# A fused decoder layer on one core: a pause of the gathers at the gates, residual rows fetched eight chunks earlier, first turns of u ahead of the last scores

## The chip, the cores and the metric

The kernel runs on one core of a Trainium2 chip, as one program. The metric is the time of one execution on the device in microseconds (us), the median of three runs. The core has five engines that the text names: TensorE (PE, matrix products), VectorE (DVE), ScalarE (ACT), GpSimd (POOL) and SyncE (SP, which here only starts transfers). Each of them issues its instructions in the order of the program; a transfer is issued on the queue of one of them and waits there, with all that stands behind it, until what it needs is ready.

## The reference, cut to what matters

One decoder layer over 256 tokens of width 1024, all in float32: a mixer (chunkwise retention and block attention, merged by gates, with an output projection and a residual add), then a retrieval of experts by product keys.

```python
def peer(h, w_q, sub_keys, u_tab, v_tab):
    q = (ht @ w_q).reshape(T, PEER_HEADS, 2, half)
    s = jnp.einsum('thcd,hcnd->thcn', q, sub_keys).astype(jnp.float32)
    s1, i1 = lax.top_k(s[:, :, 0], PEER_TOPK)
    s2, i2 = lax.top_k(s[:, :, 1], PEER_TOPK)
    ...
    top_s, pos = lax.top_k(cand_s, PEER_TOPK)
    experts = jnp.take_along_axis(cand_i, pos, axis=-1)
    gates = jax.nn.softmax(top_s, axis=-1).astype(h.dtype)
    ...
        u = u_tab[ec]
        a = jax.nn.gelu(jnp.einsum('td,thkd->thk', hc, u), approximate=False)
        return jnp.einsum('thk,thkd->td', gc * a, v_tab[ec])
...
def reference(x, ...):
        ...
        x = x + merged @ w_out[l]
        h2 = rmsnorm(x, ffn_norm_g[l])
        x = x + peer(h2, peer_w_q[l], peer_sub_keys[l], peer_u[l], peer_v[l])
```

There are 8 heads, 128 x 128 = 16384 experts with a row of `peer_u` and a row of `peer_v` each (1024 wide, 64 MB per table), and every token takes 16 experts per head.

## The kernel before, in words

The order of the work is written by hand: the program's order is each engine's order. Generators (`tasks`, `chain`) are advanced by fixed budgets between the products of PE, so that side work falls between them.

**Stages.** To about 275 us the mixer runs. Then four units of the query projection follow, each of them with an epilogue (`queries`, L567) that copies the queries to SBUF on ScalarE (L571), multiplies them by the sub-keys on PE (L580, a `side` tile of PSUM for each half of the tokens) and copies the scores out on ScalarE (L584). From there VectorE works through the choice of the best experts (`topk`).

**The tables in chunks.** Both tables are streamed whole through SBUF in 128 chunks of 128 experts (512 KB each), since 192 of the tokens are treated densely. A chunk of u is turned by 8 transposes on PE (L675, `transpose_u`; ScalarE evacuates, L676), two chunks ahead of its use (`TAHEAD`), and then multiplied with the tokens (L1178). This runs from 315 to about 695 us. The chunks of v are cut in two parts of the product's format (L141 on ScalarE gives the high part `rhi`, L142 on VectorE the remainder `rlo`) two chunks ahead, the weights likewise (`cut_w`, L1149 on ScalarE, L1150 on VectorE, every second chunk), and `block` (L1211, L1212) multiplies and sums into eight PSUM banks, one for each 128 of the output's columns, until about 985 us.

**Dense gates** (`dense_gates`, L1075). For the dense product each token needs a weight for each expert: for the 16 x 8 chosen ones the gate, else zero. The columns of chosen indices and gates are turned on PE (`columns`, L1084; ScalarE copies, L1085 and L1086); for four tokens at a time VectorE builds two sets of one-hots (L1063, `oh_buf`; L1065, `oh_more`), ScalarE scales one of them by the gates in four `factors` (L1069), and PE multiplies them (L1105, `gp`). VectorE and ScalarE evacuate the result into `W` (L1118, L1120). The generator says by `yield` how much of a budget each step costs; the main loop gives `BUDGET` 1.5 per chunk. The first group's products come two groups behind its one-hots (`LAG_G`).

**Gathers** (`gather_step`, L994). The experts' rows of 64 tokens, and the u rows of 64 more ("extra" tokens), are gathered by indirect transfers on POOL's queue (`fetch`, L942), one row per partition, into five buffers. VectorE takes the dot product of a u row (L953) one step after it is taken from the ring. For v it adds the weighted row to `vacc` (L1023). The main loop calls for 1.08 steps per chunk of u and 0.54 per chunk of v. The extra tokens' weights then go out and back through memory by POOL's queue (L964 `gx`, L969 `gates`), since the second `columns` call needs them in another layout.

**The end.** At chunk 120 (`NK - 8`) the remaining sums of gathered rows are done, and the residual rows of the first 64 tokens are loaded by ScalarE's queue (L1231) and added (L1235, L1237). At chunk 125 SP's queue stores these (L1238) and loads the other residual rows (L1241) into two buffers of the ring that otherwise holds the streamed chunks. Then, for each of the eight banks, ScalarE and VectorE add the two halves (L1248, L1249), PE turns the result back (L1254, L1255), VectorE adds the residual rows (L1256, L1257), and the result is stored (L1260, L1261).

Of the kernel before, what the change touches and what calls it, by code (L numbers as in the profile page):

```python
# [22 lines left out]
P = 128  # L23
# [20 lines left out]
BUDGET = 1.5  # L44
GSTEP = 1.6
LAG_G = 2
SCRATCH = 88
TOPK = 16
HELD = [0, 1, 2] + list(range(8, 62, 6))
# [19 lines left out]
def layer_kernel(ctx, tc, x, mix_norm_g, w_in, ret_w_branch, moba_q_gain, moba_k_gain, moba_w_branch,  # L69
# [21 lines left out]
    def side():  # L91
        return psum["side"].tile([P, 512], F32, name="side")
# [474 lines left out]
    def queries(q):  # L567
        def epi(o):
            qT = scratch[:, 4096:5120].rearrange("p (j t) -> p j t", j=4)
            for b in range(2):  # L570
                A.activation(qT[:, 2 * b:2 * b + 2, :], o[b].rearrange("p (a t) -> p a t", a=2), AF.Copy)  # L571
            yield
            if q == 0:
                yield
                yield
                assert sk_task not in tasks
            for t in range(NT):
                p = side()
                for j in range(4):
                    T.matmul(p[:, j * P:(j + 1) * P], qT[:, j, t * P:(t + 1) * P], skT[:, 4 * q + j, :],  # L580
                             start=True, stop=True)
                n0 = 512 * (2 * q + t)
                s_sb = scratch[:, n0:n0 + 512].rearrange("p (j i) -> p j i", j=4)
                A.activation(s_sb, p.rearrange("p (j i) -> p j i", j=4), AF.Copy, scale=r2[:, t:t + 1])  # L584
                (chain if t == 0 else topk_rest).append(topk(t, q, s_sb))
            yield
        return epi
# [77 lines left out]
    def transpose_u(c):  # L665

        if c < NK and c % STEP == STEP - 1 and c // STEP < NPRE:
            u_T[c] = u_raw.pop(c)
        elif c < NK:
            r = u_raw.pop(c)  # L670
            u_T[c] = hi_tile(F32)
            for q in range(2):
                p = psum["turn"].tile([P, 512], F32, name="turn")
                for k in range(4):
                    T.transpose(p[:, k * P:(k + 1) * P], r.rearrange("p (i k) -> p k i", k=KC)[:, 4 * q + k], ident)  # L675
                A.activation(u_T[c][:, 512 * q:512 * (q + 1)], p, AF.Copy)  # L676
# [145 lines left out]
            V.max_index(idx[:, 8:16], vals[:, 8:16], tmp)  # L822


    gs = {"n": 0, "u": 0, "dot": 0, "v": 0, "sum": 0, "rows": {}, "x": 0, "soft": False, "xdone": False, "later": []}

    topk_rest = []
    ready = []
# [164 lines left out]

    def gather_step():  # L994
        later()
        if gs["x"] == NX and gs["soft"]:
            weights_x()
        if gs["dot"] < NU:
            if gs["u"] < len(ready):
                fetch(peer_u[0], ready[gs["u"]])  # L1000
                gs["u"] += 1
            if gs["dot"] < gs["u"] and (gs["u"] - gs["dot"] == RING - 1 or gs["u"] == NU):
                j = ready[gs["dot"]]
                r = gs["rows"].pop(j)
                h = h2 if j < NJ else h2r[(j - NJ) // TOPK]
                after(1, partial(dot_v, j, r, h))
                gs["dot"] += 1
                if gs["dot"] == NU:
                    later()
                    A.activation(av[:, :NJ], av[:, :NJ], AF.Gelu)  # L1010
                    V.tensor_tensor(av[:, :NJ], av[:, :NJ], gg[:, :NJ], op=OP.mult)
            return
        if gs["v"] < NJ:
            fetch(peer_v[0], gs["v"])
            gs["v"] += 1
        if gs["sum"] < gs["v"] and (gs["v"] - gs["sum"] == RING or gs["v"] == NJ):
            j = gs["sum"]
            r = gs["rows"].pop(j)
            if j == 0:
                gs["acc"] = cp.tile([P, D], F32, name="vacc", tag="h2")  # L1020
                A.activation(gs["acc"], r, AF.Copy, scale=av[:, 0:1])
            else:
                V.scalar_tensor_tensor(gs["acc"], r, av[:, j:j + 1], gs["acc"], op0=OP.mult, op1=OP.add)  # L1023
            gs["sum"] += 1

    held = list(HELD)

    def hold():
# [50 lines left out]
    def dense_gates():  # L1079
# [5 lines left out]
            A.activation(tT[:, t], p[:, P:3 * P].rearrange("p (j i) -> p j i", j=2), AF.Copy)  # L1085
            A.activation(tT1[:, t], p[:, :P], AF.Copy)  # L1086

        yield 5.0
        columns(1)
        yield 0.1  # L1090
        V.tensor_scalar(niota, iota, -1.0, None, op0=OP.mult)
        oh_buf = cp.tile([P, 4, 4, NK], F32, name="oh_buf", tag="b8")
        V.tensor_copy(iota4, iota[:, :, None].to_broadcast([P, NK, 4]))
        built = []
        for n0 in range(0, ND + 4 * LAG_G, 4):
            gates_finish()
# [61 lines left out]
            h2r.append(lo_tile(F32))  # L1158
            nc.scalar.dma_start(h2r[n], h2y[n].rearrange("h i d -> (h i) d"))

    for c in range(TAHEAD):
        transpose_u(c)
    for c in range(NK):
        load_to(len(pieces) + c + TAHEAD)
        rows_x(c)
# [37 lines left out]

    o = [acc() for _ in range(KC)]
    half = P - NG
    res, late = {}, []

    def block(b, c):
        vh, vl, w = cuts[c]
# [5 lines left out]
    for c in range(NK):  # L1215
# [10 lines left out]
        if c == NK - 8:  # L1226
# [4 lines left out]
            nc.scalar.dma_start(r0[:NG], x1d[:NG, 0, :])  # L1231
            upper = hp_.tile([P, D], F32, name="rows", tag="hh", bufs=2)
            nc.gpsimd.dma_start(upper[:NG], gs["acc"][NG:])
        if c == NK - 4:
            V.tensor_tensor(r0[:NG], r0[:NG], gs["acc"][:NG], op=OP.add)  # L1235
        if c == NK - 3:
            V.tensor_tensor(r0[:NG], r0[:NG], upper[:NG], op=OP.add)  # L1237
            nc.sync.dma_start(out_flat[:NG, :], r0[:NG])  # L1238
            for i, src in enumerate((x1d[NG:, 0, :], x1d[:, 1, :])):
                res[i] = raw_tile()  # L1240
                nc.sync.dma_start(res[i][:src.shape[0]], src)  # L1241

    r0b, r1 = res[0], res[1]
    back = {}

    def add_up(b):
# [77 lines left out]
```

## Time and profile before

| what | value |
|---|---|
| three runs | 999.03, 1001.88, 1005.34 us; median 1001.88 |
| the profiled execution | 1003.14 us, span 1001.4 us (1.74 around it), mean granted clock of PE 0.992 |
| busy in the span | PE 984.5 (98%), VectorE 803.6 (80%), ScalarE 551.4 (55%), POOL 331.8 (33%) |
| moved | 309.94 MB, mean 310 GB/s |

The span is cut into the stretch before the u phase and so on by the table of windows; these are its rows, with the busy time of PE, its weight loads, VectorE, ScalarE and POOL (in brackets the count of instructions), then the granted clock, the share of the transfer engines and GB/s:

```
0.00:275.00 275.00, 272.64 (x1676) 239.43 (x1677) 190.02 (x247) 137.47 (x209) 35.13 (x41) 1.00 0.80 240
275.00:309.00 34.00, 33.93 (x280) 33.14 (x279) 29.17 (x137) 13.82 (x18) 1.77 (x3) 1.00 0.99 381
309.00:502.00 193.00, 187.07 (x1672) 186.29 (x1670) 174.08 (x603) 87.89 (x175) 96.77 (x89) 1.00 0.98 371
502.00:575.00 73.00, 73.00 (x630) 73.00 (x631) 62.17 (x108) 54.35 (x159) 36.93 (x35) 0.96 0.88 320
575.00:695.00 120.00, 119.47 (x1072) 119.28 (x1071) 83.89 (x140) 94.81 (x238) 56.46 (x58) 1.00 0.86 318
695.00:984.00 289.00, 289.00 (x2017) 289.00 (x2018) 258.11 (x254) 160.43 (x190) 104.73 (x62) 1.00 0.91 333
984.00:1001.40 17.40, 9.41 (x50) 8.27 (x48) 6.14 (x25) 2.65 (x8) 0.00 (x0) 0.75 0.36 105
```

In the rows of the time line that follow below, the first two numbers are the start from the span's begin and the duration; an arrow `out<-in` names what is written and read, with the shape; brackets at the end give the idle time of the engine ahead of the row and what ended it. Several equal instructions are put in one row with their count, and the duration then runs from the first's start to the last's end. In a list of waits stand the engine and line that waited, whom it waited for, the sum, how often and the longest.

### The profile page before, as it was taken

To read this page: it belongs to the slowest core of one execution; us is meant where nothing else is said; L and a number is where in the kernel's file an instruction comes from. 1 tells how busy PE (TensorE), PEld (TensorE's weight loads), DVE (VectorE), ACT (ScalarE), POOL (GpSimd) and SP (SyncE) were. 2 spreads that over 40 slices of the span, in tenths; PEclk is the share of its full clock that TensorE was granted. 3 is DMA by queue.
4 is the path that set the end of the run, shared out by engine and by line. 5 is a ranking of instruction groups with operands and counts; after the bars stand their busy time and mean duration, and the time that the engine had idled before them with its cause. 6 is when DMAs were issued, how large, how long until landed. Compare 5 with 4: busy or idle time off the path is not lost.

```text
span 1001.4 us, 19580 instructions
## 1 busy us (share of the span) xinstructions
PE 984.5 (98%) x7384; PEld 948.4 (95%) x7384; DVE 803.6 (80%) x1509; ACT 551.4 (55%) x992; POOL 331.8 (33%) x284
## 2 busy tenths in 40 slices
PE   9999999999999999999899999999999999999996
PEld 6887998998999999999899999999999999999996
DVE  6567665888589988999688899753989899898984
ACT  5544544535554445444477777996555555555552
POOL 2421000000204456344445545443334444333400
PEclk9999999999999999999989999999999999999998
DMA  8876777996899999999998888898999999999972
GB/s 300 240 196 183 232 241 207 280 283 225 248 398 331 407 359 344 396 362 386 369 351 312 302 295 334 325 344 287 353 348 368 340 364 351 325 373 340 374 234 73
DMA packets 105563, 309.94 MB, mean 310 GB/s; under 512 B 10956, under 2 KB 21093, under 8 KB 105342
## 3 DMA queue, kind: packets, MB, share of 16 engines
q1 hardware_dynamic: 64716, 185.48, 52.9%
q0 software_dynamic: 29936, 106.11, 29.1%
q10 hardware_dynamic: 10818, 17.11, 5.5%
q8 instruction: 58, 0.95, 0.4%
q14 instruction: 35, 0.29, 0.1%
HBM read 298.09 MB, written 12.09 MB: 310 GB/s over the span
## 4 chain that ended last, share of the span: by engine, by line
PE 86%; DVE 7%; DMA 4%; issue 1%; POOL 1%; ACT 0%; DVEq 0%; POOLq 0%; ACTq 0%
PE acc L1211 20%; PE acc L1178 15%; PE acc L1212 9%; PE turn L675 7%; PE gp L1105 4%; PE acc L232 4%; PE acc L223 4%; PE acc L233 4%; PE acc L234 4%; PE acc L225 4%; PE acc L224 4%; DVE rows L953 2%; DMA rows<-in_peer_u_dram,eg 2%; DMA rows__5234<-in_peer_u_dram,eg 1%; PE side L580 1%
## 5 line engine op out<-in xcount | busy, mean ns | idle before, releaser
L942 POOL DMA_INDIRECT rows<-in_peer_u_dram,eg x103 | 125.1, 1214 | 91.3 <-DVE rows L953 33.3
L942 POOL DMA_INDIRECT rows<-in_peer_v_dram,eg x51 | 84.6, 1660 | 118.6 <-DVE vacc L1023 111.5
L675 PE MATMUL turn<-ident,raw_ring 128*128 128x128 f32 x816 | 107.9, 276 | 0.0
L675 PEld LDWEIGHTS turn<-ident,raw_ring 128*128 128x128 f32 x816 | 99.5, 191 | 0.0
L1149 ACT ACTIVATE cw<-W 128x384 fp32r<-128x384 f32 x64 | 33.6, 526 | 81.2 <-PE acc L1212 62.8
L953 DVE SCALAR_TENSOR_TENSOR rows<-rows,h 128x1024 f32<-128x1024 f32 x51 | 62.2, 1223 | 11.6 <-DMA rows<-in_peer_u_dram,eg 11.1
L1023 DVE SCALAR_TENSOR_TENSOR vacc<-rows,av,vacc 128x1024 f32<-128x1024 f32 x50 | 64.0, 1279 | 0.0
L1120 ACT ACTIVATE W<-gp 128x512 f32<-128x512 f32 (+17 forms) x48 | 32.7, 682 | 34.5 <-DVE W L1118 26.5
L1150 DVE TENSOR_TENSOR cw<-W,cw 128x384 fp32r<-128x384 f32 x64 | 36.1, 564 | 18.8 <-ACT cw L1149 16.4
L1135 POOL TENSOR_TENSOR W<-W,gl 128x256 f32<-128x256 f32 (+16 forms) x29 | 22.5, 776 | 84.7 <-ACT gl L1134 72.1
L1063 DVE TENSOR_TENSOR oh_buf<-niota,tT 128x512 f32<-128x512 f32 x48 | 33.7, 702 | 10.6 <-PE gp L1105 8.6
L1118 DVE TENSOR_TENSOR W<-gp,W 128x280 f32<-128x280 f32 (+16 forms) x32 | 30.0, 937 | 13.4 <-PE gp L1105 9.8
L1069 ACT ACTIVATE oh_buf<-oh_more,tT 128x128 f32<-128x128 bf16 x96 | 31.8, 417 | 8.4 <-DVE oh_more L1065 8.4
L1069 ACT ACTIVATE oh_more<-oh_more,tT 128x128 f32<-128x128 bf16 x96 | 31.7, 416 | 0.0
L1105 PE MATMUL gp<-oh_buf 128*128 128x128 f32 x192 | 26.4, 282 | 5.0 <-ACT oh_buf L1069 5.0
L539 POOL DMA_DIRECT2D x1d<-xt x1 | 0.7, 657 | 89.3 <-DVE xt L521 89.3
L1105 PEld LDWEIGHTS gp<-oh_buf 128*128 128x128 f32 x192 | 24.2, 198 | 5.2 <-ACT oh_buf L1069 5.2
L148 POOL TENSOR_TENSOR gny<-va,minus_half 128x8 f32<-128x8 f32 x2 | 3.3, 1654 | 76.4 <-DVE va L441 76.4
L1178 PE MATMUL acc<-hTf,raw_ring 128*128 128x128 f32 x224 | 28.5, 282 | 0.0
L1178 PEld LDWEIGHTS acc<-hTf,raw_ring 128*128 128x128 f32 x224 | 27.4, 200 | 0.0
L1105 PE MATMUL gp<-oh_more,oh_buf 128*128 128x128 f32 x192 | 25.4, 275 | 0.0
L1105 PEld LDWEIGHTS gp<-oh_more,oh_buf 128*128 128x128 f32 x192 | 23.4, 192 | 0.0
(2198 smaller groups left out, 3562.5 us busy)
## 6 DMA issues: line engine op xcount, KB each, us to landing
raw_ring<-in_peer_v_dram SPq DMA_DIRECT2D x128, 512.0 KB
raw_ring<-in_peer_u_dram SPq DMA_DIRECT2D x102, 512.0 KB
raw_ring<-in_w_in_dram SPq DMA_DIRECT2D x52, 512.0 KB
raw_ring<-in_peer_w_q_dram SPq DMA_DIRECT2D x16, 512.0 KB
raw_ring<-turned SPq DMA_DIRECT2D x14, 512.0 KB
W<-in_peer_u_dram SPq DMA_DIRECT2D x12, 512.0 KB
raw_ring<-in_ret_w_branch_dram SPq DMA_DIRECT2D x8, 512.0 KB
raw_ring<-in_w_out_dram SPq DMA_DIRECT2D x8, 512.0 KB
```

Of the source, the lines that this page charges most:

```text
L223: T.matmul(o[t], xh[:, s], wh, start=(k == 0), stop=False)
L224: T.matmul(o[t], xh[:, s], wl, start=False, stop=False)
L225: T.matmul(o[t], xl[:, s], wh, start=False, stop=(k == kc - 1))
L675: T.transpose(p[:, k * P:(k + 1) * P], r.rearrange("p (i k) -> p k i", k=KC)[:, 4 * q + k], ident)
L942: G.indirect_dma_start(out=r, out_offset=None, in_=tab, in_offset=bass.IndirectOffsetOnAxis(ap=eg[:, j:j + 1], axis=0))
L953: V.scalar_tensor_tensor(r, r, 1.0, h, op0=OP.mult, op1=OP.mult, accum_out=av[:, j:j + 1])
L1023: V.scalar_tensor_tensor(gs["acc"], r, av[:, j:j + 1], gs["acc"], op0=OP.mult, op1=OP.add)
L1069: A.activation(o1[:, j], o1b[:, :, j], AF.Copy, scale=tT[:, t, 1, k + j:k + j + 1])
L1105: T.matmul(p[:, j * P:(j + 1) * P], o2, o1, start=True, stop=True)
L1178: T.matmul(pa[:, n:n + NA], uT[:, k * P:(k + 1) * P], hTf[:, k], start=(c % 2 == 0 and k == 0), stop=(k == KC - 1), skip_group_check=True)
L1211: T.matmul(o[b][:, :2 * ND], vh[:, n], w, start=(c == 0), stop=False, skip_group_check=True)
L1212: T.matmul(o[b][:, :ND], vl[:, n], w[:, :ND], start=False, stop=(c == NK - 1), skip_group_check=True)
```

## The change

Three parts. (1) The generator of the gates allocates its buffer, sets a pause of three gather steps (`gs["pause"]`) and yields 3.0 in place of 5.0 before its first columns; two constant tables that it built itself (`niota`, `iota4`) are built before the query units' loop. (2) In the last query unit the first two chunks of u are turned ahead of the unit's scores, in `side` tiles of PSUM, and no longer after them. (3) The residual rows of the end are loaded at chunk 120 on ScalarE's queue, right behind the load that stands there already: `r1` into a buffer of the gathered rows, `r0b` into the one-hots' buffer `oh_more`; the two loads on SP's queue at chunk 125 and their buffers of the ring are gone.

```diff
--- before.py
+++ after.py
@@ -44,6 +44,7 @@
 BUDGET = 1.5
 GSTEP = 1.6
 LAG_G = 2
+PAUSE = 3
 SCRATCH = 88
 TOPK = 16
 HELD = [0, 1, 2] + list(range(8, 62, 6))
@@ -574,6 +575,10 @@
                 yield
                 yield
                 assert sk_task not in tasks
+            if q == 3:
+
+                for c in range(TAHEAD):
+                    transpose_u(c)
             for t in range(NT):
                 p = side()
                 for j in range(4):
@@ -670,7 +675,7 @@
             r = u_raw.pop(c)
             u_T[c] = hi_tile(F32)
             for q in range(2):
-                p = psum["turn"].tile([P, 512], F32, name="turn")
+                p = psum["turn"].tile([P, 512], F32, name="turn") if "turn" in psum else side()
                 for k in range(4):
                     T.transpose(p[:, k * P:(k + 1) * P], r.rearrange("p (i k) -> p k i", k=KC)[:, 4 * q + k], ident)
                 A.activation(u_T[c][:, 512 * q:512 * (q + 1)], p, AF.Copy)
@@ -822,7 +827,7 @@
             V.max_index(idx[:, 8:16], vals[:, 8:16], tmp)
 
 
-    gs = {"n": 0, "u": 0, "dot": 0, "v": 0, "sum": 0, "rows": {}, "x": 0, "soft": False, "xdone": False, "later": []}
+    gs = {"n": 0, "u": 0, "dot": 0, "v": 0, "sum": 0, "rows": {}, "x": 0, "soft": False, "xdone": False, "later": [], "pause": 0}
 
     topk_rest = []
     ready = []
@@ -993,6 +998,9 @@
 
     def gather_step():
         later()
+        if gs["pause"] > 0:
+            gs["pause"] -= 1
+            return
         if gs["x"] == NX and gs["soft"]:
             weights_x()
         if gs["dot"] < NU:
@@ -1023,6 +1031,8 @@
                 V.scalar_tensor_tensor(gs["acc"], r, av[:, j:j + 1], gs["acc"], op0=OP.mult, op1=OP.add)
             gs["sum"] += 1
 
+    V.tensor_scalar(niota, iota, -1.0, None, op0=OP.mult)
+    V.tensor_copy(iota4, iota[:, :, None].to_broadcast([P, NK, 4]))
     held = list(HELD)
 
     def hold():
@@ -1085,12 +1095,11 @@
             A.activation(tT[:, t], p[:, P:3 * P].rearrange("p (j i) -> p j i", j=2), AF.Copy)
             A.activation(tT1[:, t], p[:, :P], AF.Copy)
 
-        yield 5.0
+        oh_buf = cp.tile([P, 4, 4, NK], F32, name="oh_buf", tag="b8")
+        gs["pause"] = PAUSE
+        yield 3.0
         columns(1)
         yield 0.1
-        V.tensor_scalar(niota, iota, -1.0, None, op0=OP.mult)
-        oh_buf = cp.tile([P, 4, 4, NK], F32, name="oh_buf", tag="b8")
-        V.tensor_copy(iota4, iota[:, :, None].to_broadcast([P, NK, 4]))
         built = []
         for n0 in range(0, ND + 4 * LAG_G, 4):
             gates_finish()
@@ -1158,8 +1167,6 @@
             h2r.append(lo_tile(F32))
             nc.scalar.dma_start(h2r[n], h2y[n].rearrange("h i d -> (h i) d"))
 
-    for c in range(TAHEAD):
-        transpose_u(c)
     for c in range(NK):
         load_to(len(pieces) + c + TAHEAD)
         rows_x(c)
@@ -1203,7 +1210,6 @@
 
     o = [acc() for _ in range(KC)]
     half = P - NG
-    res, late = {}, []
 
     def block(b, c):
         vh, vl, w = cuts[c]
@@ -1231,16 +1237,16 @@
             nc.scalar.dma_start(r0[:NG], x1d[:NG, 0, :])
             upper = hp_.tile([P, D], F32, name="rows", tag="hh", bufs=2)
             nc.gpsimd.dma_start(upper[:NG], gs["acc"][NG:])
+            r1 = hp_.tile([P, D], F32, name="rows", tag="hh", bufs=2)
+            r0b = oh_more.rearrange("p a b i -> p (a b i)")
+            nc.scalar.dma_start(r1, x1d[:, 1, :])
+            nc.scalar.dma_start(r0b[:half], x1d[NG:, 0, :])
         if c == NK - 4:
             V.tensor_tensor(r0[:NG], r0[:NG], gs["acc"][:NG], op=OP.add)
         if c == NK - 3:
             V.tensor_tensor(r0[:NG], r0[:NG], upper[:NG], op=OP.add)
             nc.sync.dma_start(out_flat[:NG, :], r0[:NG])
-            for i, src in enumerate((x1d[NG:, 0, :], x1d[:, 1, :])):
-                res[i] = raw_tile()
-                nc.sync.dma_start(res[i][:src.shape[0]], src)
-
-    r0b, r1 = res[0], res[1]
+
     back = {}
 
     def add_up(b):
```

How this moves instructions shows at three places (the changed program's lines are up to ten higher; names with two underscores and a number are single buffers).

VectorE, from the softmax of the gates (`sm`, `gates`) to the first one-hots, before:

```order
L908 TENSOR_TENSOR gates<-gates,sm 128x128
L953 SCALAR_TENSOR_TENSOR rows,av<-rows,rlo__3251 128x1024 x3
L953 SCALAR_TENSOR_TENSOR rows__5234,av<-rows__5234,rlo__3251 128x1024
L1091 TENSOR_SCALAR niota<-iota 128x128
L1093 CAST iota_2576<-iota 128x512
L1063 TENSOR_TENSOR oh_buf<-niota,tT 128x512
L1065 TENSOR_TENSOR oh_more<-iota_2576,tT_2577 128x512
L953 SCALAR_TENSOR_TENSOR rows,av<-rows,rlo__3251 128x1024
```

and of the change:

```order
L913 TENSOR_TENSOR gates<-gates,sm 128x128
L958 SCALAR_TENSOR_TENSOR rows,av<-rows,rlo__3253 128x1024 x2
L1073 TENSOR_TENSOR oh_buf<-niota,tT 128x512
L1075 TENSOR_TENSOR oh_more<-iota_2576,tT_2577 128x512
L1073 TENSOR_TENSOR oh_buf<-niota,tT 128x512
L1075 TENSOR_TENSOR oh_more<-iota_2576,tT_2577 128x512
L1073 TENSOR_TENSOR oh_buf<-niota,tT 128x512
L1075 TENSOR_TENSOR oh_more<-iota_2576,tT_2577 128x512
L1127 TENSOR_TENSOR W<-gp,W 128x4x68
L958 SCALAR_TENSOR_TENSOR rows,av<-rows,rlo__3253 128x1024
```

Of four dots ahead of the first one-hots two are left, and three groups of one-hots follow without a dot between them.

PE at the same place, from the columns to the first product of the gates, before:

```order
L1084 MATMUL turn<-ident,i12f 128x128 x2
L1084 MATMUL turn<-ident,gates 128x128
L1178 MATMUL acc<-hTf,rhi__5294 128x128 x8
L675 MATMUL turn<-ident,raw_ring 128x128 x8
L1178 MATMUL acc<-hTf,rhi__5319 128x128 x8
L1105 MATMUL gp<-oh_buf 128x128 x4
```

and of the change:

```order
L1094 MATMUL turn<-ident,i12f 128x128 x2
L1094 MATMUL turn<-ident,gates 128x128
L680 MATMUL turn<-ident,raw_ring 128x128 x8
L1185 MATMUL acc<-hTf,rhi__5269 128x128 x8
L1185 MATMUL acc<-hTf,rhi__5295 128x128 x8
L1114 MATMUL gp<-oh_buf 128x128 x4
```

Between columns and first product stand two chunks' products and one turn in both; in the change the columns stand one chunk earlier in the u phase.

ScalarE around chunk 120 of v, before:

```order
L1149 ACTIVATE cw<-W 128x2x192
L1231 DMA rows__10353<-x1d 64x1024
L141 ACTIVATE rhi__10358<-raw_ring 128x1024
L141 ACTIVATE rhi__10379<-raw_ring 128x1024
L1149 ACTIVATE cw<-W 128x2x192
```

and of the change:

```order
L1158 ACTIVATE cw<-W 128x2x192
L1237 DMA rows__10355<-x1d 64x1024
L1242 DMA rows<-x1d 128x1024
L1243 DMA oh_more<-x1d 64x1024
L142 ACTIVATE rhi__10363<-raw_ring 128x1024
L142 ACTIVATE rhi__10384<-raw_ring 128x1024
L1158 ACTIVATE cw<-W 128x2x192
```

Two loads more stand ahead of the cut of chunk 123 (`rhi__10358` before, `rhi__10363` now). On VectorE, in the same stretch, the last sum of gathered rows stood one pair of chunks earlier before; in the change three sums (`vacc`) stand behind the `cw` of this pair.

## The prediction

> **What bounds the kernel now.** I read the list of waits by engine first, because the page gives PE 984.5 us of a 1001.4 us span: only what PE waits for, or what slows PE itself, can move the end. Of PE:
>
> ```profile
> PE gp L1105 <- ACT oh_buf L1069: 5.0, 1, 5.0
> PE acc L1254 <- DVE turned L1249: 4.3, 3, 3.4
> PE turn L675 <- ACT W L584: 0.8, 1, 0.8
> ```
>
> Three single events hold 10.1 us, and the diff touches the place of each. The table by stretches shows that the two long ones cost more than their idle time (the column behind the busy times is the granted clock):
>
> ```profile
> 500.00:502.00 2.00, 0.14 (x1) 0.14 (x1) 2.00 (x5) 0.61 (x2) 1.70 (x2) 0.76 1.03 410
> 502.00:504.00 2.00, 2.00 (x10) 2.00 (x11) 2.00 (x5) 2.00 (x7) 1.31 (x2) 0.50 0.96 369
> 504.00:506.00 2.00, 2.00 (x11) 2.00 (x10) 2.00 (x5) 1.16 (x4) 1.14 (x1) 0.50 1.01 350
> 506.00:508.00 2.00, 2.00 (x12) 2.00 (x11) 2.00 (x5) 1.75 (x5) 0.00 (x1) 0.53 0.87 313
> ...
> 986.00:988.00 2.00, 1.24 (x10) 1.01 (x8) 0.00 (x0) 0.66 (x2) 0.00 (x0) 1.00 0.94 256
> 988.00:990.00 2.00, 0.00 (x0) 0.00 (x0) 0.12 (x1) 0.00 (x0) 0.00 (x0) 0.79 0.49 193
> 990.00:992.00 2.00, 1.32 (x5) 1.29 (x6) 1.76 (x8) 0.00 (x0) 0.00 (x0) 0.50 0.00 0
> ```
>
> Behind the wait at the gates PE runs at half clock until about 507.9. The clock missing over the four rows from 500 is 0.48 + 1.00 + 1.00 + 0.94 = 3.4 us of full speed; some 0.4 of it fell on time in which PE stood anyway, so 3.0 us are lost. Wait and clock together: 5.0 + 3.0 = 8.0 us. At the end the same follows the wait of 3.4.
>
> **Gathering pauses, gates earlier.** PE, then VectorE and ScalarE, around that wait:
>
> ```profile
> 489.26 1.05 PE L675 MATMUL turn<-ident,raw_ring 128*128 128x128 f32 x8
> 491.93 0.38 PE L1084 MATMUL turn<-ident,i12f 128*128 128x128 f32 x2
> 494.93 1.95 PE L1178 MATMUL acc<-hTf,rhi__5319 128*128 128x128 f32 x16
> 501.86 2.07 PE L1105 MATMUL gp<-oh_buf 128*128 128x128 f32 x8 [4.98 <-ACT oh_buf L1069]
> ```
>
> ```profile
> 489.61 0.29 DVE L908 TENSOR_TENSOR gates<-gates,sm 128x128 f32<-128x128 f32 x1
> 491.03 1.22 DVE L953 SCALAR_TENSOR_TENSOR rows<-rows,rlo__3251 128x1024 f32<-128x1024 f32 x1 [1.13 <-DMA rows<-in_peer_u_dram,eg]
> ...
> 493.60 1.23 DVE L953 SCALAR_TENSOR_TENSOR rows<-rows,rlo__3251 128x1024 f32<-128x1024 f32 x1 [1.33 <-DMA rows<-in_peer_u_dram,eg]
> ...
> 498.71 1.23 DVE L953 SCALAR_TENSOR_TENSOR rows__5234<-rows__5234,rlo__3251 128x1024 f32<-128x1024 f32 x1 [1.33 <-DMA rows__5234<-in_peer_u_dram,eg]
> ...
> 500.34 0.69 DVE L1063 TENSOR_TENSOR oh_buf<-niota,tT 128x512 f32<-128x512 f32 x1
> ```
>
> ```profile
> 501.39 1.32 ACT L1069 ACTIVATE oh_buf<-oh_more,tT 128x128 f32<-128x128 bf16 x4 [8.38 <-DVE oh_more L1065]
> ```
>
> The one-hots don't wait for their own data (the columns left PE at 492). They stand on VectorE behind four dots, and each dot waits for a gathered row; rows land about every 2.55 us (491.03, 493.60, ..., 498.71). The change leaves two dots ahead of the first one-hots, takes the two constants away from here, and lets the columns go one chunk of PE's work earlier, to 489.26. There the columns wait for `gates` (489.61 + 0.29 = 489.90), some 0.5 us with the hop. PE then has three columns (0.33 from start to start), one turn (0.89: half of the pitch left by a chunk's 2.68 after a product of 1.79) and two products (1.79 each, 1.95 with the drain of the last): ready at 490.2 + 0.89 + 1.79 + 1.79 = 494.7. VectorE is through the second dot at 493.60 + 1.23 = 494.83; one-hots take from 500.34 to ScalarE's 501.39, that is 1.05, and from there to the product 0.47: gp at 496.4. PE waits 1.7 there, and 0.3 more because the last of four factors comes 1.32 after the first while a gp of four takes 0.89. Loss 0.5 + 1.7 + 0.3 = 2.5 instead of 8.0: a gain of **5.5** if the clock stays full, and 2.5 if it falls again for the same 3.0.
>
> What decides the clock, only the nearest rows can say. The 0.78 us wait at 312 was followed by full clock; the 4.98 and the 3.4 were followed by half. Before the drop at the end (about 989.2, from the row with 0.79) PE had idled since 987.2, 2.0 us, with about as much idle in the stretch as work. So waits of 0.5 and 2.0, two products apart, lie between the cases, and nearer to the end's: whether the clock falls depends on when they come. I take half the price, 1.5: a gain of **4.0**, ends 2.5 and 5.5, and nothing if the two rows land later than now.
>
> [...]
>
> What else moves with this: three gather steps (a fetch of about 0.9 to 1.3 us on POOL and a dot of 1.23 on VectorE each) come later, and so all later ones. That costs nothing as long as PE waits for no gather, and PE's list of waits names none for a gathered row. The constants (0.4 on VectorE, from the last dot's end at 499.94 to 500.34) go to where the query units run, where PE's list shows no wait for VectorE; I take nothing.
>
> **First turns of u ahead of the last scores.** The rows at the place:
>
> ```profile
> 309.42 2.46 PE L580 MATMUL side<-skT,W 128*128 128x128 f32 x16
> 312.66 2.95 PE L675 MATMUL turn<-ident,W 128*128 128x128 f32 x24 [0.78 <-ACT W L584]
> 315.45 1.73 PE L1178 MATMUL acc<-hTf,rhi__3160 128*128 128x128 f32 x14
> ```
>
> ```profile
> 309.62 0.60 ACT L571 ACTIVATE W<-acc 128x512 f32<-128x512 f32 x1 [0.26 <-PE acc L234]
> 311.09 1.51 ACT L584 ACTIVATE W<-side,r 128x512 f32<-128x512 f32 x2 [0.87 <-PE side L580]
> 313.46 1.09 ACT L676 ACTIVATE rhi__3160<-turn 128x512 f32<-128x512 f32 x2 [0.85 <-PE turn L675]
> ```
>
> The 16 scores stretch over 2.46 because the second half needs the queries that ScalarE writes until 310.22; then the first turn waits for ScalarE to empty the scores. With 16 turns put first (0.89 per eight, so 1.8) that first wait is covered: turns 309.3 to 311.1, scores (1.8 without a wait) to 312.9. ScalarE now empties four turn tiles (1.09 per two) ahead of the scores: 310.2 to 312.3, scores to 313.8. The third set of turns waits for that, about 1.0 (instead of 0.78), takes 0.89, and the first product starts at 314.7 instead of 315.45: **0.75** gained. Ends: nothing, if the wait only moves, and 1.4, if both stretches vanish.
>
> **Residual rows eight chunks ahead.** Now:
>
> ```profile
> 989.88 0.29 DVE L1256 TENSOR_TENSOR raw_ring<-raw_ring,acc 128x128 f32<-128x128 f32 x1 [3.88 <-DMA raw_ring<-x1d]
> ```
>
> ```profile
> 985.49 0.33 PE L1254 MATMUL acc<-ident,turned 128*128 128x128 f32 x1 [0.24 <-DVE turned L1249]
> ...
> 986.31 0.27 PE L1254 MATMUL acc<-ident,turned 128*128 128x128 f32 x1
> ```
>
> ```profile
> 997.24 0.33 PE L1254 MATMUL acc<-ident,turned 128*128 128x128 f32 x1 [0.59 <-DVE turned L1249]
> ```
>
> The first add of a block waits 3.88 for its residual rows; everything behind it stands, and then PE runs at half clock. With the rows there, eight blocks go at the pace of the first two (0.82): the eighth turn back at 985.49 + 7 x 0.82 = 991.2 instead of 997.24, **6.0** gained. VectorE's part per block (0.35 + 0.28 + 0.27 = 0.9 in durations, 0.67 from start to start) keeps up.
>
> But the new loads go out on ScalarE's queue, behind the last sums of gathered rows, and ahead of the cut of chunk 123:
>
> ```profile
> 970.67 0.52 ACTq L1231 DMA_DIRECT2D rows__10353<-x1d  x1
> 971.29 1.06 ACT L141 ACTIVATE rhi__10358<-raw_ring 128x1024 fp32r<-128x1024 f32 x1 [0.39 <-DMA rows<-vacc]
> ```
>
> ```profile
> 966.89 1.28 DVE L1023 SCALAR_TENSOR_TENSOR vacc<-rows,av,vacc 128x1024 f32<-128x1024 f32 x1
> ...
> 971.00 0.56 DVE L1150 TENSOR_TENSOR cw<-W,cw 128x384 fp32r<-128x384 f32 x1 [0.56 <-ACT cw L1149]
> 972.38 1.23 DVE L142 TENSOR_TENSOR rlo__10359<-raw_ring,rhi__10358 128x1024 fp32r<-128x1024 f32 x1 [0.82 <-ACT rhi__10358 L141]
> ```
>
> ```profile
> 977.05 0.36 PE L1211 MATMUL acc<-cw,rhi__10358 128*128 128x384 f32 x1
> ```
>
> Three steps late, the gathers leave three sums for one stretch: on VectorE from 971.47 (the start of `cw` 971.00 plus 0.47, as 966.42 to 966.89) three times 1.2 (1.28 less the overlap with the next), until 975.07. The load into the buffer of the last gathered row waits on ScalarE for that; two issues of 0.52 follow, and only then the cut, 976.3 to 977.35 (now 971.29), then its remainder on VectorE until 978.6. PE wants the first at 977.05 and the second 0.2 later: **1.3** us lost. Ends: nothing (were the sums done earlier), and 4.3 with a fall of the clock, which 1.3 us of idle make unlikely.
>
> **Sum.** 0.75 + 4.0 + 6.0 - 1.3 = 9.45 us off the profiled span of 1001.4, whose execution took 1003.14, 1.26 above the median. Off the median of 1001.88 that is **992.4 us**.
>
> **Rivals.**
> (1) The clock does not fall at the gates and the hold-up of chunk 123 is smaller (0.3): 0.75 + 5.5 + 6.0 - 0.3 = 12 us off, 990. For it: the only rows with half clock follow waits of over 3.4. [...]
> (2) The two rows still ahead of the one-hots land later than now, or the clock falls at both places: 0.75 + 2.5 + 6.0 - 4.3 = 5 us off, 997. For it: rows have come at an even 2.55 since 491, so their pace is the transfers', and nothing in the change quickens those two.
> (3) The pause does nothing (the fetches catch up, and dots wait as before): 0.75 + 6.0 - 1.3 = 5.5 off, 996.4. Against: the order of VectorE has two dots fewer there.
> (4) Slower: the weights of the extra tokens come late. They go out and back in two transfers on POOL's queue, and the last columns are turned on PE when they are back:
>
> ```profile
> 580.47 0.85 POOL L964 DMA_DIRECT2D gx<-av  x1
> ...
> 587.31 2.25 POOL L969 DMA_DIRECT2D gates<-gx  x4
> ```
>
> ```profile
> 607.37 0.38 PE L1084 MATMUL turn<-ident,i12f 128*128 128x128 f32 x2
> ```
>
> Between the end of the second issue (589.56) and the columns lie 17.8 us. Three steps later (at 1.08 per chunk of 3.3 us, 9.2 us) leaves 8.6, and 14.8 from the first hop's start. If one hop took 12.05 us, as the slowest gathered row in the chain of waits does,
>
> ```profile
> 486.64 12.05 DMA rows__5234<-in_peer_u_dram,eg
> ```
>
> PE would wait 2 x 12.05 + 2.25 - 14.8 = 11.5 us and lose 3.0 of clock: 992.4 + 14.5 = 1007. It makes the kernel slower from a hop of 9.4 us on. Against: the first hop is done within 6.84 now, since POOL issues the second without a wait.
>
> **Chances.** Forecast (991 to 995) 0.55; rival 1 0.22; rival 2 and 3 together 0.18; rival 4 0.04, and 0.01 for the rest. One per cent, 10 us, is about what a measurement can tell from none, and the forecast lies just inside: a third of its own cases and nearly all of rival 1 are beyond 991.9, 0.39 in all; slower by over 1% only a part of rival 4, 0.03; the rest, 0.58, within. Range 988.5 to 997: it takes in the forecast, rivals 1 to 3 but for their outer parts, and leaves rival 4 out.
>
> **What would show it.** Right: in PE's list gp no longer waits over 2.5 us, acc at the turn back under 1; the stretch after the gates begin has its clock above 0.75 in the mean; a wait of PE for ScalarE's or VectorE's cut of chunk 123 of 1 to 2 us appears, which now doesn't exist; the first product of u starts at 314.7 on the old scale; the last turn back comes 6 us less after the first. Wrong: a wait of gp of 4 us or more (the rows still rule), half clock behind the 1.3 us wait, a wait of the last columns, or a new wait at the step from u to v because the last dots of u come three steps later.

## The result and the profile after

| | median of ten runs | lowest to highest | profiled span |
|---|---|---|---|
| before | 1002.66 us | 999.03 to 1005.34 | 1001.4 us |
| the change | 997.11 us | 994.62 to 999.20 | 995.7 us |

The ratio is 0.9943 (95% interval 0.9928 to 0.9959): 5.7 us less, where 9.45 were forecast. On the median that the forecast started from, that is 1001.88 x 0.9943 = 996.2 us instead of 992.4. The gain is real and six tenths of what was summed up.

The list of PE's waits after the change, from the longest on (engine and line, whom it waited for, total, times, longest):

```profile
PE turn L1094 <- DVE gates L913: 1.6, 1, 1.6
...
PE acc L1217 <- ACT rhi__10363 L142: 1.3, 1, 1.3
PE side L585 <- ACT W L572: 1.3, 1, 1.3
PE gp L1114 <- ACT oh_buf L1079: 0.9, 1, 0.9
PE acc L1218 <- DVE rlo__10364 L143: 0.8, 1, 0.8
...
PE acc L1260 <- DVE turned L1255: 0.6, 2, 0.3
```

The waits of 5.0 and 3.4 are gone. Shorter ones stand at places which the prediction spoke of (columns, gp, both parts of the cut of chunk 123). One, 1.3 us of an earlier query unit's scores (`side`, L585), was not foreseen.

**The gates.** PE's time line, with idle time in brackets:

```profile
489.98 0.38 PE L1094 MATMUL turn<-ident,i12f 128*128 128x128 f32 x2
491.93 0.33 PE L1094 MATMUL turn<-ident,gates 128*128 128x128 f32 x1 [1.56 <-DVE gates L913]
...
494.79 1.95 PE L1185 MATMUL acc<-hTf,rhi__5295 128*128 128x128 f32 x16
497.65 1.39 PE L1114 MATMUL gp<-oh_buf 128*128 128x128 f32 x8 [0.91 <-ACT oh_buf L1079]
```

The idle time is 1.56 + 0.91, as the estimate had it (2.5 in all), and the products keep their full speed (granted clock 1.00): eight of gp take 1.39, where before they took 2.07 at half clock (0.50).

**The end.** The first, second and last turn back:

```profile
985.52 0.33 PE L1260 MATMUL acc<-ident,turned 128*128 128x128 f32 x1 [0.24 <-DVE turned L1255]
...
986.36 0.28 PE L1260 MATMUL acc<-ident,turned 128*128 128x128 f32 x1
...
991.73 0.33 PE L1260 MATMUL acc<-ident,turned 128*128 128x128 f32 x1 [0.34 <-DVE turned L1255]
```

From first to last 6.21 us, before 997.24 - 985.49 = 11.75.

**Chunk 123.** PE, then ScalarE:

```profile
974.37 0.44 PE L1217 MATMUL acc<-cw,rhi__10363 128*128 128x384 f32 x1 [1.32 <-ACT rhi__10363 L142]
975.63 0.53 PE L1218 MATMUL acc<-cw,rlo__10364 128*128 128x192 f32 x1 [0.82 <-DVE rlo__10364 L143]
975.96 0.57 PE L1217 MATMUL acc<-cw,rhi__10363 128*128 128x384 f32 x1
...
979.38 0.36 PE L1217 MATMUL acc<-cw,rhi__10384 128*128 128x384 f32 x1
```

```profile
966.21 0.53 ACT L1158 ACTIVATE cw<-W 128x384 fp32r<-128x384 f32 x1 [1.32 <-PE acc L1218]
968.62 0.51 ACTq L1237 DMA_DIRECT2D rows__10355<-x1d  x1
971.26 0.33 ACTq L1242 DMA_DIRECT2D rows<-x1d  x1
971.62 1.53 ACTq L1243 DMA_DIRECT2D oh_more<-x1d  x1
973.26 1.06 ACT L142 ACTIVATE rhi__10363<-raw_ring 128x1024 fp32r<-128x1024 f32 x1 [6.53 <-issue]
```

ScalarE computes nothing for 6.5 us: its queue holds the loads, and the second of them leaves at 971.26, when VectorE ends its third sum (968.62 + 2.60 = 971.2). PE waits 1.32 for the high part, 0.82 for the remainder, and then products that take 0.36 take 0.57, at a granted clock of 0.50 from 975.59 to 979.00.

**Where the 5.5 us come from.** The same events on the two time lines give a ledger; the last product of the query projection stood at 309.11 and stands at 310.54, the first of u at 315.45 and 316.18, the `cw` of chunk 118 at 965.79 and 961.62, the first turn back at 985.49 and 985.52, the last at 997.24 and 991.73:

| stretch | forecast | measured |
|---|---|---|
| up to the end of the query projection | 0 | -1.43 (lost) |
| first turns of u | +0.75 | +0.70 |
| gates, up to chunk 118 of v | +4.0 | +4.90 |
| chunk 118 of v to the first turn back | -1.3 | -4.20 |
| turns back | +6.0 | +5.54 |
| sum | +9.45 | +5.51 |

The unforeseen wait of 1.3 us makes up most of the first row. The `cw` of chunk 118 is the cut of weights on ScalarE that is issued in that chunk's turn of the loop.

### The profile page after: what moved, and what is told of

Read it like the earlier page. It is cut to its first block, busy times and chain, and to the rows that moved or that the text cites. A ratio compares the mean times of both kernels' runs of the same rounds, so it can differ in the third digit from the quotient of the medians.

```text
span 995.7 us, 19593 instructions
## 1 busy us (share of the span) xinstructions
PE 981.7 (99%) x7384; PEld 944.9 (95%) x7384; DVE 803.1 (81%) x1509; ACT 552.6 (55%) x993; POOL 337.2 (34%) x285
## 4 chain that ended last, share of the span: by engine, by line
PE 83%; DVE 9%; DMA 3%; ACT 2%; issue 1%; ACTq 1%; POOL 1%; DVEq 0%; POOLq 0%
PE acc L1217 20%; PE acc L1185 15%; PE acc L1218 9%; PE turn L680 6%; PE gp L1114 4%; PE acc L233 4%; PE acc L235 4%; PE acc L234 4%; PE acc L224 4%; PE acc L226 4%; PE acc L225 4%; DVE rows L958 3%; DMA rows<-in_peer_u_dram,eg 3%; PE side L585 1%; DVE W L874 1%
## 5 line engine op out<-in xcount | busy, mean ns | idle before, releaser
L947 POOL DMA_INDIRECT rows<-in_peer_v_dram,eg x51 | 88.9, 1743 | 123.7 <-DVE vacc L1031 108.5
L1144 POOL TENSOR_TENSOR W<-W,gl 128x256 f32<-128x256 f32 (+17 forms) x30 | 25.1, 838 | 81.8 <-ACT gl L1143 70.2
L1129 ACT ACTIVATE W<-gp 128x512 f32<-128x512 f32 (+18 forms) x48 | 33.0, 687 | 31.1 <-DVE W L1127 26.2
L1127 DVE TENSOR_TENSOR W<-gp,W 128x280 f32<-128x280 f32 (+17 forms) x32 | 29.7, 927 | 13.9 <-PE gp L1114 7.4
```

Of the source, the lines that this page charges most:

```text
L947: G.indirect_dma_start(out=r, out_offset=None, in_=tab, in_offset=bass.IndirectOffsetOnAxis(ap=eg[:, j:j + 1], axis=0))
```

## The experiments

Ten runs of eight kernels follow (e12 and e13 repeat e10 and e1). The kernel before was timed beside each group on the same chip, and every ratio is to it.

### Is it the loads ahead of the cut? (e1_loads_behind_cut)

The whole change, but its two loads are one chunk later:

```diff
             nc.gpsimd.dma_start(upper[:NG], gs["acc"][NG:])
+        if c == NK - 7:
             r1 = hp_.tile([P, D], F32, name="rows", tag="hh", bufs=2)
             r0b = oh_more.rearrange("p a b i -> p (a b i)")
             nc.scalar.dma_start(r1, x1d[:, 1, :])
             nc.scalar.dma_start(r0b[:half], x1d[NG:, 0, :])
```

> The whole change, but the two residual loads are issued one chunk later on the same queue (ScalarE's), behind the cut of chunk 123 instead of ahead of it. Theory H (the loads wait for the third sum of gathered rows and hold the cut of chunk 123 up; this took the 4.2 us that the whole change lost between chunk 122 and 124, idle 2.3 and half clock 1.9): PE has no wait for either part of the cut of chunk 123, the turn back still runs at 0.8 us per block, and the time is 5.5 + 4.2 = 9.7 us under before, a ratio of 0.990 (0.988 to 0.992). Rival S (the three sums in a row on VectorE are the cost, not the queue): the remainder of the cut is still late, PE waits 1 us or more for it, 6 to 7 us under before. Rival L (loads one chunk later come too late for the first add): PE waits again at the turn back, 7 us under before or less.

Measured: 992.92 us against 1003.2, ratio 0.9901 (0.9887 to 0.9915). ScalarE's time line:

```profile
965.60 0.52 ACTq L1237 DMA_DIRECT2D rows__10355<-x1d  x1
966.21 1.06 ACT L142 ACTIVATE rhi__10360<-raw_ring 128x1024 fp32r<-128x1024 f32 x1 [2.50 <-DVE vacc L1031]
968.24 0.33 ACTq L1243 DMA_DIRECT2D rows<-x1d  x1
968.60 1.53 ACTq L1244 DMA_DIRECT2D oh_more<-x1d  x1
970.26 1.06 ACT L142 ACTIVATE rhi__10384<-raw_ring 128x1024 fp32r<-128x1024 f32 x1 [2.98 <-PE acc L1218]
```

The cut of chunk 123 now runs at 966.21, while the loads still wait for the last sum, and PE has no wait for either part of it. The three sums in a row are still there, so rival S falls; the turn back keeps its pace, so rival L falls. What remains is a wait of 0.8 for the weights' cut (`cw`), which the loads still push back on ScalarE. So the loss is not gone to the last: from the `cw` of chunk 118 to the first turn back this trace takes 979.50 - 958.59 = 20.91 us, the change 23.90 and the kernel before 19.70.

### The end alone (e2_end_alone)

The kernel before with the third part only: the loads stand ahead of the cut as in the change.

```diff
+            r1 = hp_.tile([P, D], F32, name="rows", tag="hh", bufs=2)
+            r0b = oh_more.rearrange("p a b i -> p (a b i)")
+            nc.scalar.dma_start(r1, x1d[:, 1, :])
+            nc.scalar.dma_start(r0b[:half], x1d[NG:, 0, :])
...
-            for i, src in enumerate((x1d[NG:, 0, :], x1d[:, 1, :])):
-                res[i] = raw_tile()
-                nc.sync.dma_start(res[i][:src.shape[0]], src)
```

> The kernel before with only the end's part (residual loads at chunk 120 on ScalarE's queue, ahead of the cut of chunk 123). Here the last sum of gathered rows is done one pair of chunks earlier, so the loads have nothing to wait for. Theory H: no wait of PE for the cut of chunk 123, the turn back quickened by 5.5 us: 5.5 under before, ratio 0.9945 (0.993 to 0.996). Rival Q (three issues on ScalarE's queue hold the cut up by themselves): a wait of 1 to 2 us at chunk 123 here too, and 1.3 to 4 us under before.

Measured: 996.42 against 1003.2, ratio 0.9941 (0.9921 to 0.9960), so this part alone gains as much as the whole change. ScalarE:

```profile
969.60 0.51 ACTq L1230 DMA_DIRECT2D rows__10353<-x1d  x1
970.24 0.52 ACTq L1235 DMA_DIRECT2D rows<-x1d  x1
970.79 0.64 ACTq L1236 DMA_DIRECT2D oh_more<-x1d  x1
971.53 1.06 ACT L141 ACTIVATE rhi__10361<-raw_ring 128x1024 fp32r<-128x1024 f32 x1 [1.69 <-DMA rows<-vacc]
```

The same three issues in the same place, none of them waiting, and the cut starts 2.2 us after `cw` (969.31) instead of 7.0; PE waits for neither part, and the `cw` of chunk 118 to the first turn back takes 984.42 - 964.73 = 19.69, as before. So rival Q falls: it is the combination that holds up. The pause at the gates makes all gathers three steps late, and so leaves three sums in front of loads that the end's part put in front of the cut.

### The gates alone (e3_gates_alone)

```diff
-        yield 5.0
+        oh_buf = cp.tile([P, 4, 4, NK], F32, name="oh_buf", tag="b8")
+        gs["pause"] = PAUSE
+        yield 3.0
```

with the constants and the test in `gather_step` as in the change, and none of its other parts.

> The kernel before with only the gates' part (pause of three gather steps, earlier columns, constants built earlier). Theory: about 5.0 us under before when the clock stays full at the gates (ratio 0.995), 2.5 when it falls there (0.9975). At the end the residual rows come as before on SP's queue, so the wait of 3.4 and the half clock stay. Rival G (later gathers cost elsewhere, at chunk 120 or at the step from u to v): under 2 us gained, with a new wait of PE in its list.

Measured: 998.48 against 1003.2, ratio 0.9944 (0.9926 to 0.9963). In the trace the columns waited 2.13 for the gates, and behind that the clock fell (0.50 from 493.10 to 496.52):

```profile
490.17 0.38 PE L1090 MATMUL turn<-ident,i12f 128*128 128x128 f32 x2
492.69 0.33 PE L1090 MATMUL turn<-ident,gates 128*128 128x128 f32 x1 [2.13 <-DVE gates L909]
492.85 1.70 PE L676 MATMUL turn<-ident,raw_ring 128*128 128x128 f32 x8
```

Eight turns take 1.70 instead of 1.05. The median lies by the case of a full clock, though the clock fell in the traced execution. The wait at the end stays (3.6 at the longest). One wait is new, 1.0 us for ScalarE's `W` ahead of the gates; with 4.7 us gained, rival G falls all the same. The gates and the end alone multiply to 0.9941 x 0.9944 = 0.9885, and together (with the first turns) they gave 0.9943: 5.8 us are lost where they meet, of which the stretch with chunk 123 accounts for 4.2 in the trace (it takes 19.69 here too) and the width of the intervals can account for the rest.

### The first turns alone (e4_turns_alone)

```diff
+            if q == 3:
+
+                for c in range(TAHEAD):
+                    transpose_u(c)
```

> The kernel before with only the first turns of u ahead of the last scores. Theory: 0.7 us under before, ratio 0.9993, which is below what the runs can tell; in the trace the first product of u starts 5.5 us after the last product of the query projection instead of 6.2. The 1.3 us wait of an earlier unit's scores in the whole change is put down to a transfer of query weights that landed late in that execution and is absent here or in other traces. Rival: that wait belongs to this part, is there again, and the time is 0.6 us over before.

Measured: 1003.24 against 1003.2, ratio 0.9998 (0.9982 to 1.0013): nothing that can be told from none. In the trace the first product of u starts 315.17 - 309.53 = 5.64 us after the last one of the projection, as in the whole change, against 6.34 before. The unforeseen wait of an earlier unit's scores is 0.8 here. In the other traces it is 0 to 0.4 without this part and 0 to 2.1 with it; nothing of the part is issued before that place, and both executions of one kernel with it have none (e10, e12). What makes it long stays open; in the change, the cut ahead of it on ScalarE waits for a transfer of query weights that landed later than before (1.42 until 281.77, before 0.38 until 280.12).

### The pause (e5_no_pause) and the place of the columns (e10, e11)

From e1's kernel, `PAUSE = 0` (e5), or the generator's first `yield 5.0` (e10), or both (e11). With the columns late, two dots stand ahead of the one-hots with the pause and four without; with early columns, two and three.

> The kernel of e1 (whole change, loads behind the cut of chunk 123) with the pause set to 0 and the earlier columns kept. Theory P (the one-hots stand on VectorE behind dots whose rows land every 2.55 us, so each dot left ahead of them costs 2.55): one dot more stands ahead, gp waits 2.5 us longer than in e1 (0.7 there), 3 us or more, and the clock may fall behind it for one or two stretches of 1.7: 995.5 to 999, ratio 0.993 to 0.996. Rival C (the earlier columns and constants are the gain, the pause is not): as e1, 993, ratio 0.990.

Measured: 997.37 against 1001.97, ratio 0.9951 (0.9934 to 0.9968). VectorE and PE:

```profile
493.97 1.23 DVE L958 SCALAR_TENSOR_TENSOR rows<-rows,rlo__3253 128x1024 f32<-128x1024 f32 x1 [1.33 <-DMA rows<-in_peer_u_dram,eg]
...
496.53 1.23 DVE L958 SCALAR_TENSOR_TENSOR rows<-rows,rlo__3253 128x1024 f32<-128x1024 f32 x1 [1.32 <-DMA rows<-in_peer_u_dram,eg]
```

```profile
499.19 2.08 PE L1114 MATMUL gp<-oh_buf 128*128 128x128 f32 x8 [3.49 <-ACT oh_buf L1079]
```

One row more to wait for, 2.56 us, and gp waits 3.49 instead of 0.7; the clock falls (0.50 from 498.1 to 504.9, 6.8 us). The time is in the range that theory P gave: with early columns the pause is the gain.

> The kernel of e1 with the generator's first step at 5.0 as before, so that the columns stand one chunk of PE's work later; pause and earlier constants are kept. Theory P: the one-hots still stand behind two dots only, PE has 2.7 us of products more in front of gp, so PE waits neither for the gates nor for gp, and the time is that of e1 or up to 1 us less, ratio 0.989 to 0.990. Rival C: the earlier columns are the gain, and without them gp waits 3 us or more: 996 or over.

Measured: 989.45 against 1001.97, ratio 0.9878 (0.9857 to 0.9899), a little under the range of theory P; rival C falls. PE runs through the place with no wait at all:

```profile
491.61 0.38 PE L1094 MATMUL turn<-ident,i12f 128*128 128x128 f32 x2
...
494.61 1.95 PE L1185 MATMUL acc<-hTf,rhi__5317 128*128 128x128 f32 x16
496.39 1.17 PE L1114 MATMUL gp<-oh_buf 128*128 128x128 f32 x8
```

> The kernel of e10 (whole change, loads behind the cut of chunk 123, columns one chunk later) with the pause set to 0: the fourth corner beside e1 (early columns, pause), e5 (early, no pause) and e10 (late, pause). Theory P (the pause takes two dots of 2.55 us each out of the way, the place of the columns only decides whether they wait for the gates): four dots stand ahead of the one-hots as before, gp waits 3 to 5 us, the clock falls for one or two stretches of 1.7, 995 to 998, ratio 0.993 to 0.996. Rival K (the constants built earlier and the late columns did it): as e10, ratio 0.988.

Measured: 994.67 against 1003.13, ratio 0.9922 (0.9898 to 0.9947), between theory P and rival K and in the range of neither. gp waits 4.85 in the trace, about as before the change (4.98). In the same group the kernel with the pause took 993.18: by the runs alone the pause is worth 1.5 us there, within their scatter; by the traces (spans of 995.8 and 991.2) it is 4.6, but the traced execution is the slowest of e11's six. So with late columns the wait is shown and its price is not, and no run takes the early constants back alone.

### Late and early columns once more (e12, e13)

The kernels of e10 and e1 without any edit, in the group of e11.

> The kernel of e10 once more, beside e1's on one chip: theory: PE has no wait at the gates, ratio 0.987 to 0.990. If the columns have no slack to gain, e1 and this agree within 0.1%.

> The kernel of e1 once more, beside e10's on one chip. Theory: early columns wait for the gates in some executions (0 to 3 us in the traces so far, by how late gathered rows land on VectorE between 400 and 420), so it is 1 to 3 us slower than late columns and scatters more, ratio 0.989 to 0.992.

Measured: late 993.18 against 1003.13, ratio 0.9910 (0.9885 to 0.9935), early 994.04, ratio 0.9915 (0.9891 to 0.9940). In this group the runs tell no difference between the two places of the columns, so both expectations are missed: late columns lie above their range, and early ones are 0.9 us behind instead of 1 to 3. The gap between e1 and e10 in their first runs is not an advantage of the columns' place that the repeat confirms. PE had no wait for gates or gp in e12. In the traced execution it did worse than in e10 at the scores, where ScalarE kept the turns waiting 1.86 us (0.78 in e10), the clock fell (0.50 from 317.1 to 320.5), and the first product of u came at 317.63 instead of 315.13:

```profile
316.37 1.46 PE L680 MATMUL turn<-ident,W 128*128 128x128 f32 x8 [1.86 <-ACT W L589]
317.63 0.63 PE L1185 MATMUL acc<-hTf,rhi__3116 128*128 128x128 f32 x2
```

One difference between the two kernels stands in the traces of both groups, and it is at the end, not at the gates: from the `cw` of chunk 118 to the first turn back e1 and e13 take 20.91, e10 and e12 19.82 and 19.83. The load into `oh_more` holds ScalarE's queue for 1.53 and 1.54 in the former, for 0.46 in the latter, here in e10:

```profile
967.47 0.46 ACTq L1244 DMA_DIRECT2D oh_more<-x1d  x1
```

Both versions beat the kernel before and, by their middle values in all four timings (0.9878 to 0.9915), the change as it stood (0.9943); in their first runs their intervals lie wholly below its interval, in the second they overlap its lower end.

### The early turns, taken out of e1 (e7_no_early_turns)

```diff
-            if q == 3:
-
-                for c in range(TAHEAD):
-                    transpose_u(c)
```

> The kernel of e1 without the first turns of u ahead of the last scores (they stand behind them as before). Theory: the part is worth 0.7 us or nothing: ratio 0.990 to 0.991 as e1, and the first product of u starts 6.2 us after the query projection's last product instead of 5.5. Rival: the earlier start is passed on through the choice of experts to the gates, so that without it gp waits longer and the clock falls: 2 us or more slower than e1, ratio 0.992 or over.

Measured: 993.63 against 1001.97, ratio 0.9912 (0.9884 to 0.9940): as e1 within the scatter, and the first product of u starts 6.20 after the last of the projection, as expected. In this trace the columns waited 2.77 for the gates, which VectorE finished late; the clock did not fall (1.00 from 484 to 500). The rival is not excluded: the interval reaches past 0.992, and of the six traces with early columns the two without this part wait longest for the gates (2.13 in e3 and 2.77 here; with it 1.56 or less).

## Why the prediction was right in direction and 4 us short

**The gates (forecast +4.0, measured +4.90): mechanism right.** The one-hots were behind dots that waited for rows. e5 and e11 put the dots back and the wait came back by the step of the rows. The price of 8.0 was read from one execution, though: e2 and e4 have the gates of the kernel before, and gp waits 3.3 and 3.1 there instead of 5.0. The sum's idle time (2.5) was right, but its distribution was not: 1.56 at the columns instead of 0.5, and 0.91 at gp instead of 1.7 + 0.3, because the gates themselves were later than on the old line. The half price for the clock was the error of the term: the clock stayed full, near the upper end of 5.5. By the rows below that was luck of position more than of length. What was not seen at all is that the earlier columns buy nothing that the runs can tell: with the pause gp came early enough, and e10 ran with the columns where they had been.

**The end (+6.0, measured +5.54): right.** Rows in time, eight blocks at 0.8 to 1.0 a block (the pitch of the first two, 0.82, is that of a pair; between pairs it is 0.97).

**Chunk 123 (-1.3, measured -4.20): the mis-sized step.** The place, the chain (third sum, two issues, cut, remainder) and even the wait were foreseen. Two sizes failed. The second issue was priced at 0.52 as the first, and it took 1.53, 1.0 more, so the cut came later and PE stood 2.14 us instead of 1.3. And the prediction called a fall of the clock one "which 1.3 us of idle make unlikely"; it fell to 0.50 for 3.41 us, which is 1.7 us more; half clock behind this wait stood in the list of what would show the prediction wrong. The remaining 0.4 the trace doesn't split further. e1 moved the loads behind the cut, and 3.0 of the 4.2 us were gone in its trace (20.91 instead of 23.90); in the runs it is 0.9901, and 0.9915 when repeated, against 0.9943, which is 4.2 and 2.8 us of a thousand. With either of the two parts alone (e2, e3) the stretch takes 19.69, so the loss belongs to their meeting.

**First turns (+0.75, measured +0.70 in the trace): right in size, and not to be seen in the time** (e4 0.9998, e7 as e1).

**Of the rivals**, the first came closest in its gates (no fall of the clock there), the second in its price at chunk 123, named there as the end 4.3. The third and the fourth did not occur: the order kept its two dots, and the weights of the extra tokens were back in time (in e13 the last columns waited 0.4 for them, nowhere else). The fourth's price does not come out of its rows: from the first issue (580.47) to the columns (607.37) there are 26.9 us, 17.7 after the 9.2 are taken off, not 14.8, so its wait would have been 8.7 and not 11.5.

**The total.** 996.2 lies within the range of 988.5 to 997, near its end. Part of that is luck: the gates brought 0.9 more than forecast and so covered some of the 2.9 that chunk 123 took on top of its 1.3 and of the 1.4 that no term had.

**When does the clock fall?** The fall decided two terms. In the trace of the kernel before the clock changed at 501.05, 507.87, 989.15, 995.97 and 999.39, that is 2, 141, 2 and 1 times 3.413 us apart, and in that of the change at 975.59, 979.00 and, just behind its last instruction, 996.07, 1 and 5 times. The rows cut the time lines into such stretches, counted from a change of each trace's clock: PE's busy time in each stretch (second number), then the granted clock; of the kernel before, of the change, and of e3 and e4 at the gates:

```profile
497.63:501.05 3.42, 0.00 (x0) 1.00 1.03 411
501.05:504.46 3.41, 2.60 (x12) 0.50 1.00 378
504.46:507.87 3.41, 3.41 (x18) 0.50 0.91 324
507.87:511.29 3.42, 3.42 (x33) 1.00 0.73 218
...
985.73:989.15 3.42, 1.51 (x12) 1.00 0.89 272
989.15:992.56 3.41, 1.88 (x9) 0.50 0.01 2
```

```profile
490.90:494.31 3.41, 2.38 (x21) 1.00 1.04 416
494.31:497.73 3.42, 2.51 (x23) 1.00 1.02 408
...
972.18:975.59 3.41, 1.31 (x8) 1.00 0.90 221
975.59:979.00 3.41, 3.37 (x13) 0.50 0.42 87
```

```profile
489.69:493.10 3.41, 1.28 (x12) 1.00 1.01 396
493.10:496.52 3.42, 3.42 (x19) 0.50 1.03 413
```

```profile
494.53:497.94 3.41, 2.07 (x19) 1.00 1.02 408
497.94:501.35 3.41, 1.61 (x12) 1.00 1.03 408
501.35:504.77 3.42, 3.42 (x19) 0.50 0.93 332
```

In these rows a stretch in which PE was busy for 1.61 us or less (47%) was followed by half clock; one with 2.07 (61%) or more was not. A stretch at half clock with 2.60 or less kept it for another, one with 3.37 or more gave full clock back (in e11 one with 2.96 did). One stretch does not fit. In e7, counted back in whole stretches from the next change of its clock (993.91, just behind its last instruction), one with 1.48 us (43%) kept full clock:

```profile
488.74:492.15 3.41, 1.48 (x14) 1.00 1.03 410
492.15:495.57 3.42, 2.59 (x23) 1.00 1.03 412
```

So the busy time of a stretch goes with the falls but does not settle them, and what else counts stays open. At a clock of 0.50 a stretch of 3.413 us has 1.7 us less of full speed, and the falls in these rows lasted one stretch (the change, e3 and e4) or two (the kernel before). The falls went with the place of a wait of about 2 us beside its length: 2.14 at chunk 123 lay all but whole in one stretch, which kept 1.31 us of work, and the clock fell, as behind e3's 2.13 (1.28 of work); 2.47 at the gates were split by borders, 2.38 and 2.51 of work were left in two of the stretches, and it didn't. The prediction read waits by their length.

## What to carry to other kernels

When a load is moved to another engine's queue, list what it waits for after all other parts of the change have been made, and what stands behind it there: each part here was free of this loss alone (19.69 us for the stretch with chunk 123 in e2 and e3, 23.90 in the change), and their meeting cost nearly as much as one of them gained (5.8 us; the end alone gained 5.9). Here the loads that had to wait were better issued behind the work that the next stage needs (one chunk later), which left 1.2 of the 4.2 us. And a pause that cleared the way for the critical instruction was worth more than starting earlier: with early columns 0.9901 (e1) against 0.9951 without it (e5), while late and early columns gave 0.9910 and 0.9915 (e12 and e13).

## What the runs showed of the hardware that was not expected

- The prediction went by the length of waits. In these traces the clock fell to 0.50 after stretches of 3.413 us in which PE was busy for 47% or less (1.61 us in e4), with one exception (1.48, 43%, in e7), and not after those of 61% and more (2.07 in e4). It came back to 1.00 after a stretch at half clock that was busy for 87% or more (2.96 in e11); behind one of 76% (2.60 in the kernel before) it did not.
- Issuing one of the residual loads on ScalarE's queue took between 0.33 and 1.56 us in these traces. The longest are those of the load into `oh_more` (64 rows) in the four traces with pause and early columns (the change, e1, e7 and e13: 1.53 to 1.56); in e2, e5, e10, e11 and e12 the same load took 0.46 to 0.70. Why is open.
